# A hybrid decoder layer: the first piece of the input projections ordered by kinds of parts, and the keys' second copies made by DMA

## The chip, the core and the metric

The kernel runs on one core of a Trainium2 chip. A core has a matrix engine (TensorE, PE in the profile; PEld is its loading of weights), a vector engine (VectorE, DVE), an engine for activation functions (ScalarE, ACT), a general engine (GpSimd, POOL) and an engine that only issues transfers (SyncE, SP). Each takes its instructions in a fixed order and waits at semaphores for the others. ACT, POOL and SP issue DMA transfers, which all run on the same 16 DMA engines. Matrix products go to PSUM, which is divided into banks of 128 x 512 words; the other data lie in SBUF, 128 partitions wide.

The metric is the time of one execution on the device in microseconds (us); smaller is better. A change is compared with the kernel before on the same chip.

## What is computed

One layer with 1024 tokens, 16 learned meta tokens ahead of them, model width 1024, in float32. Cut to what matters here:

```python
u = rmsnorm(h, g_pre_mix)                   # h: 1040 x 1024
z = u @ w_in
q, k, v, xr, yr = jnp.split(z, [512, 640, 768, 1280], axis=-1)
attn = sliding_window_attention_with_sinks(q, k, v, sinks)    # 8 heads of 64, 2 key heads, window 128
xr = causal_depthwise_conv(xr, conv_w, conv_b)
rec = gelu(yr) * rg_lru(xr, ...)            # gates, then a recurrence over the tokens
h = h + rmsnorm(concat([attn, rec]) @ w_out, g_post_mix)
f = square(relu(rmsnorm(h, g_pre_ffn) @ w_ff1)) @ w_ff2       # width 4096
out = (h + rmsnorm(f, g_post_ffn))[16:]
```

## The kernel before

**Products in parts.** Every float32 operand of a product is split into a high part (a reduced float32 that PE multiplies quickly) and a low part (what is left). A product is then three matmuls: high by high, high by low, low by high. `mm3` (L121) issues the three in a row for each chunk of 128 of the inner dimension: L123, L124 and L125 in the profile. The high part is made by ACT (L95 for weights, L116 for u), the low part by DVE from the source and the high part (L98, L117), so DVE's instruction always follows ACT's.

**The opening.** The 1040 rows come in four blocks, `ALL` (L218): 272 columns of the transposed activations, then three of 256. For a block, `norm_rows` (L197) squares each tile of 128 rows on ACT (L200), POOL adds epsilon and takes the power -0.5 (L158, L164), and DVE scales the rows (L202). `transposed` (L235) transposes the scaled rows on PE (L242) chunk by chunk, eight chunks, into banks of three kinds (pt, o, s; two of each), and splits each chunk into the high and low parts of u (L116, L117). Then four projections with 128 output columns follow (L349 to L352): K, V, the first Q pair and the first X chunk. `project` (L205) runs 24 matmuls into a bank of kind acc, of which there are two, and a sink empties it. The key's sink `put_k` (L300) does for each of the two key heads: the high part on ACT (L303), a second copy of it on the other 64 partitions on DVE (L304), and the low part on DVE (L305). The scores need the high part on both halves, since the stationary operand holds q's high part on one half and q's low part on the other (L447, L451). The meta tokens' keys are kept apart in `km`; the other keys lie in `khh` (high, both halves) and `kl` (low, with the other half set to zero by POOL at L298).

**After it.** Scores and softmax (`scores`, L432: L467 and L480 on DVE, L82 on ACT) and the use of the values (`attend`, L486) run for four Q pairs and two halves of the tokens. The remaining projections (`fill_q`, `fill_x`, `fill_y`) are put between them with a lower priority, so that PE has work while a softmax runs. Then come the gates and the recurrence, the output projection, and the feed-forward part with seven products in place of eight.

**What sets the order.** The program is written in order of priority, and a planner that runs before the kernel is built turns it into one fixed list of instructions for each engine: it takes, by its own estimate of the times, the ready instruction of the highest priority. `behind` (L105) adds an order between two instructions of one engine without a semaphore. A tile of a kind (`slot`, `bank`) waits for an earlier tile of that kind to be done with.

Of the kernel before, what the change touches and what calls it, by code (L numbers as in the profile page):

```python
# [10 lines left out]
F32R = mybir.dt.float32r  # L11
AF = mybir.ActivationFunctionType
ALU = mybir.AluOpType
# [3 lines left out]
P = 128  # L17
D = 1024
KC = D // P
# [18 lines left out]
def hybrid_layer(  # L38
# [30 lines left out]
    def f32(ap):  # L69
        return ap.bitcast(F32)  # L70
# [34 lines left out]
    def behind(name, *inss):  # L105
        for ins in inss:
            tc.add_manual_dep(
                ins, name,
                mybir.DependencyInfo(
                    mybir.DependencyClass.NoSync, mybir.DependencyReason.DATA  # L110
                ),
                reason="order",
            )

    def split_scaled(hi, lo, src, scale):
        nc.scalar.activation(hi, src, AF.Copy, scale=scale)  # L116
        nc.vector.scalar_tensor_tensor(  # L117
            lo, src, scale, f32(hi), op0=ALU.mult, op1=ALU.subtract
        )

    def mm3(dst, lhs, rhs, start, stop):  # L121
        (lh, ll), (rh, rl) = lhs, rhs
        nc.tensor.matmul(dst, lh, rh, start=start, stop=False, skip_group_check=True)  # L123
        nc.tensor.matmul(dst, lh, rl, start=False, stop=False, skip_group_check=True)  # L124
        nc.tensor.matmul(dst, ll, rh, start=False, stop=stop, skip_group_check=True)  # L125


    ident = const.tile([P, P], F32, name="ident")
# [26 lines left out]
    def rstd_of(ssq_parts, n=P):  # L155
        ms = small.tile([P, 1], F32, name="ms", tag="ms")
        if len(ssq_parts) == 1:
            nc.gpsimd.tensor_scalar(ms[:n], ssq_parts[0], EPS, None, op0=ALU.add)  # L158
        else:
            nc.vector.scalar_tensor_tensor(  # L160
                ms[:n], ssq_parts[0], EPS, ssq_parts[1], op0=ALU.add, op1=ALU.add
            )
        rs = small.tile([P, 1], F32, name="rs", tag="rs")
        nc.gpsimd.tensor_tensor(rs[:n], ms[:n], half_pow[:n], op=ALU.pow)  # L164
        return rs[:n]


    def load_cols(cols, tag="ws"):
# [25 lines left out]
    u = [pair("a", [P, TT]) for _ in range(KC)]  # L194
    RMS_SC = 1.0 / math.sqrt(D)

    def norm_rows(src, n):  # L197
        xn = slot("d", [P, D])
        ssq = small.tile([P, 1], F32, name="ssq", tag="ssq")
        nc.scalar.activation(xn[:n], src, AF.Square, scale=RMS_SC, accum_out=ssq[:n])  # L200
        rs = rstd_of([ssq[:n]], n)
        nc.vector.tensor_scalar(xn[:n], src, rs, None, op0=ALU.mult)  # L202
        return xn

    def project(w, pieces, sink):  # L205
        wh, wl = w
        for t0, n in pieces:
            acc = bank("acc")
            for kc in range(KC):
                uh, ul = u[kc]  # L210
                mm3(
                    acc[:, :n], (wh[:, kc, :], wl[:, kc, :]),
                    (uh[:, t0 : t0 + n], ul[:, t0 : t0 + n]),
                    kc == 0, kc == KC - 1,
                )
            sink(acc[:, :n], t0, n)

    ALL = [(0, 272), (272, 256), (528, 256), (784, 256)]  # L218
    REAL2 = [(16, 512), (528, 512)]

    zero = slot("ws", [P, 512])
    nc.vector.memset(zero, 0.0)
# [12 lines left out]
    def transposed(b, xn):  # L235
        t0, n = ALL[b]
        for kc in range(KC):
            flip[0] += 1
            pt = bank(("pt", "o", "s")[flip[0] % 3])
            o = 0  # L240
            for s, m in xn:
                nc.tensor.transpose(  # L242
                    pt[:, o : o + m], s[:m, kc * P : (kc + 1) * P], ident[:m, :m]
                )
                o += m
            uh, ul = u[kc]
            split_scaled(
                uh[:, t0 : t0 + n], ul[:, t0 : t0 + n], pt[:, :n],
                g_mix_col[:, kc : kc + 1],
            )  # L250

    def fetch(cols, tag="raw"):
        raw = slot(tag, [P, KC, P])
# [20 lines left out]
    rx = fetch([(X_COL, P)], "e")  # L274
    for i in range(4, 8):
        load_x(i)
    wk = split_w(rk, "b")
    wv = split_w(rv, "b")
    transposed(0, xn)
    wq = split_w(rq)  # L280
    wx = split_w(rx)
    nsink = const.tile([P, 8], F32, name="nsink")
    nc.sync.dma_start(nsink, attn_sinks[0].partition_broadcast(P))
    prm_r = slot("d", [8, 512])
# [2 lines left out]
        nc.sync.dma_start(prm_r[4 + i : 5 + i, :], src)  # L287

    khh = [slot("b", [P, T], F32R) for _ in range(2)]
    kl = [slot("b", [P, T], F32R) for _ in range(2)]

    vk = [slot("b", [P, 8, P], F32R) for _ in range(2)]
    HALF = (slice(0, HD), slice(HD, P))
    vt = slot("c", [P, TT])
    for h in range(2):
        nc.gpsimd.memset(f32(kl[h][HALF[1 - h]]), 0.0)  # L298

    def put_k(hh, lo, src):  # L300
        for h in range(2):
            r, o = HALF[h], HALF[1 - h]
            nc.scalar.copy(hh[h][r], src[r])  # L303
            nc.vector.tensor_copy(hh[h][o], src[r])  # L304
            nc.vector.tensor_tensor(lo[h][r], src[r], f32(hh[h][r]), op=ALU.subtract)  # L305

    def sink_k(acc, t0, n):
        o = 0
        if t0 == 0:
            m = slice(0, NMETA)  # L310
            put_k(
                [km[:, 0, m], km[:, 1, m]], [km[:, 2, m], km[:, 3, m]], acc[:, m]
            )
            o = NMETA
        c = slice(t0 + o - NMETA, t0 - NMETA + n)
        put_k(
            [khh[0][:, c], khh[1][:, c]], [kl[0][:, c], kl[1][:, c]], acc[:, o:]
        )

    def sink_v(acc, t0, n):  # L320
        nc.scalar.copy(vt[:, t0 : t0 + n], acc)

    def new_q():

        q = pair("b", [P, T])

        def sink_q(acc, t0, n):
            c = slice(t0 - NMETA, t0 - NMETA + n)
            for h in range(2):
                r, o = HALF[h], HALF[1 - h]  # L330
                split_scaled(q[h][r, c], q[h][o, c], acc[r], HD ** -0.5)

        return q, sink_q

    def new_x(tag="d"):
# [4 lines left out]

        return xr, sink_x

    q0, sink_q0 = new_q()
# [938 lines left out]
```

## Time and profile before

| what | value |
|---|---|
| median of 3 runs | 973.48 us (972.43 to 975.89) |
| the profiled execution | 972.95 us |
| span of its profile, first to last instruction | 971.1 us |
| PE busy | 953.7 us, 98% |
| DVE busy | 674.6 us, 69% |
| ACT busy | 502.0 us, 52% |
| POOL busy | 82.4 us, 8% |
| granted clock of PE | 0.999 |

The span is 1.85 us shorter than the execution's own time. A row of the timeline gives the start and the length of an instruction in us, the engine, the line of the code, the operation, what it writes and reads, and the shapes; in square brackets stands how long its engine was idle before it and what ended that. A matmul's length includes the way through the array, so the distance between two starts tells its cost in a stream. PE counts as busy at whatever rate it runs.

### The profile page before, as it was taken

To read this page: it belongs to the slowest core of one execution; us is meant where nothing else is said; L and a number is where in the kernel's file an instruction comes from. 1 tells how busy PE (TensorE), PEld (TensorE's weight loads), DVE (VectorE), ACT (ScalarE), POOL (GpSimd) and SP (SyncE) were. 2 spreads that over 40 slices of the span, in tenths; PEclk is the share of its full clock that TensorE was granted. 3 is DMA by queue.
4 is the path that set the end of the run, shared out by engine and by line. 5 is a ranking of instruction groups with operands and counts; after the bars stand their busy time and mean duration, and the time that the engine had idled before them with its cause. 6 is when DMAs were issued, how large, how long until landed. Compare 5 with 4: busy or idle time off the path is not lost.

```text
span 971.1 us, 12490 instructions
## 1 busy us (share of the span) xinstructions
PE 953.7 (98%) x4782; PEld 803.0 (83%) x4782; DVE 674.6 (69%) x997; ACT 502.0 (52%) x809; POOL 82.4 (8%) x109
## 2 busy tenths in 40 slices
PE   6999999999999999999999999999999999999997
PEld 6999999888878887888888878888888888888786
DVE  6679997775976686665645465468557676779694
ACT  6646673567844554343555556555433344445350
POOL 4100000000002100000000000000111000003152
PEclk9999999999999999999999999999999999999999
DMA  9002001012234466576522264323678765548923
GB/s 296 23 1 66 23 23 44 23 48 64 84 119 144 159 207 209 173 251 209 198 87 87 97 206 125 114 87 114 172 176 198 186 224 187 184 163 195 223 80 87
DMA packets 88219, 130.13 MB, mean 134 GB/s; under 512 B 13624, under 2 KB 52552, under 8 KB 88160
## 3 DMA queue, kind: packets, MB, share of 16 engines
q1 hardware_dynamic: 79792, 107.33, 33.4%
q0 software_dynamic: 7792, 20.45, 10.1%
q10 hardware_dynamic: 576, 1.57, 0.4%
q8 instruction: 37, 0.61, 0.2%
q14 instruction: 22, 0.18, 0.1%
HBM read 110.46 MB, written 18.87 MB: 133 GB/s over the span
## 4 chain that ended last, share of the span: by engine, by line
PE 89%; DVE 4%; DMA 3%; issue 2%; ACT 1%; POOL 0%; SPq 0%; POOLq 0%; DVEq 0%; ACTq 0%
PE ps_acc L124 11%; PE ps_acc L123 11%; PE ps_acc L125 11%; PE ps_s L125 6%; PE ps_pt L123 6%; PE ps_s L124 6%; PE ps_pt L125 6%; PE ps_s L123 6%; PE ps_pt L124 6%; PE ps_o L124 5%; PE ps_o L123 5%; PE ps_o L125 5%; PE ps_o L506 2%; PE ps_pt L495 1%; DMA raw<-in_w_ff_dram 1%
## 5 line engine op out<-in xcount | busy, mean ns | idle before, releaser
L95 ACT CAST ws<-raw 128x1024 fp32r<-128x1024 f32 (+1 forms) x69 | 70.7, 1024 | 126.6 <-PE ps_o L124 48.8
L98 DVE TENSOR_TENSOR ws<-raw,ws 128x1024 fp32r<-128x1024 f32 (+1 forms) x70 | 83.5, 1194 | 59.6 <-ACT ws L95 59.5
L123 PE MATMUL ps_acc<-a,ws 128*128 128x256 f32 (+2 forms) x272 | 90.5, 333 | 0.6 <-DVE b L305 0.6
L124 PE MATMUL ps_acc<-a,ws 128*128 128x256 f32 (+2 forms) x272 | 89.8, 330 | 0.0
L125 PE MATMUL ps_acc<-a,ws 128*128 128x256 f32 (+2 forms) x272 | 89.4, 329 | 0.0
L98 DVE TENSOR_TENSOR b<-b,b 128x1024 fp32r<-128x1024 f32 (+2 forms) x48 | 57.6, 1201 | 24.7 <-PE ps_o L124 17.1
L95 ACT CAST ws<-e 128x1024 fp32r<-128x1024 f32 x43 | 45.0, 1046 | 55.3 <-PE ps_o L124 28.1
L95 ACT CAST b<-b 128x1024 fp32r<-128x1024 f32 (+2 forms) x48 | 49.4, 1030 | 42.8 <-DVE b L788 40.0
L98 DVE TENSOR_TENSOR ws<-e,ws 128x1024 fp32r<-128x1024 f32 x43 | 52.6, 1222 | 21.6 <-ACT ws L95 21.6
L123 PEld LDWEIGHTS ps_acc<-a,ws 128*128 128x128 f32 x272 | 51.2, 188 | 4.9 <-DVE b L305 0.8
L125 PEld LDWEIGHTS ps_acc<-a,ws 128*128 128x128 f32 x272 | 51.2, 188 | 4.6
L124 PEld LDWEIGHTS ps_acc<-a,ws 128*128 128x128 f32 x272 | 51.2, 188 | 3.9
L164 POOL TENSOR_TENSOR rs<-ms,half_pow 128x1 f32<-128x1 f32 (+1 forms) x31 | 21.3, 692 | 356.5 <-DVE ms L160 355.1
L123 PE MATMUL ps_acc<-ws,b 128*128 128x512 f32 (+1 forms) x120 | 46.3, 386 | 0.4 <-ACT ws L95 0.4
L124 PE MATMUL ps_acc<-ws,b 128*128 128x512 f32 (+1 forms) x120 | 46.5, 388 | 0.2 <-DVE ws L98 0.2
L125 PE MATMUL ps_acc<-ws,b 128*128 128x512 f32 (+1 forms) x120 | 46.2, 385 | 0.0
L123 PE MATMUL ps_pt<-ws,b 128*128 128x512 f32 x112 | 44.1, 394 | 0.0
L124 PE MATMUL ps_pt<-ws,b 128*128 128x512 f32 x112 | 44.1, 394 | 0.0
L125 PE MATMUL ps_pt<-ws,b 128*128 128x512 f32 x112 | 44.0, 393 | 0.0
L123 PE MATMUL ps_s<-ws,b 128*128 128x512 f32 x110 | 43.4, 395 | 0.0
L124 PE MATMUL ps_s<-ws,b 128*128 128x512 f32 x110 | 43.3, 393 | 0.0
L125 PE MATMUL ps_s<-ws,b 128*128 128x512 f32 x110 | 43.3, 393 | 0.0
(381 smaller groups left out, 2690.1 us busy)
## 6 DMA issues: line engine op xcount, KB each, us to landing
raw<-in_w_ff_dram SPq DMA_DIRECT2D x62, 512.0 KB, 4.0
e<-in_w_ff_dram SPq DMA_DIRECT2D x45, 512.0 KB, 3.6
d<-in_w_ff_dram SPq DMA_DIRECT2D x12, 512.0 KB, 3.8
s_dram<-d POOLq DMA_DIRECT2D x12, 512.0 KB, 3.9
raw<-in_w_in_dram SPq DMA_DIRECT2D x9, 512.0 KB, 3.6
c<-in_x_dram SPq DMA_DIRECT2D x8, 512.0 KB, 8.5
d<-in_x_dram SPq DMA_DIRECT2D x8, 512.0 KB, 4.6
out_dram<-raw SPq DMA_DIRECT2D x8, 512.0 KB, 2.6
```

What stands on the lines that cost most here:

```text
L95: nc.scalar.copy(hi, src)
L98: low = nc.vector.tensor_tensor(lo, src, f32(hi), op=ALU.subtract).ins
L123: nc.tensor.matmul(dst, lh, rh, start=start, stop=False, skip_group_check=True)
L124: nc.tensor.matmul(dst, lh, rl, start=False, stop=False, skip_group_check=True)
L125: nc.tensor.matmul(dst, ll, rh, start=False, stop=stop, skip_group_check=True)
L164: nc.gpsimd.tensor_tensor(rs[:n], ms[:n], half_pow[:n], op=ALU.pow)
L495: nc.tensor.transpose(pt[:, o : o + P], sn[h][:, 2 * bp + i, s * P : (s + 1) * P], ident,)
L506: nc.tensor.matmul(po[:, oc : oc + n], v, p_[:, pc : pc + n], start=first and k == 0, stop=last and k == 1, skip_group_check=True,)
```

## The change

In the first block the four projections no longer run chunk by chunk. A new function `part` issues the eight matmuls of one kind for a block: kind 0 is high by high, 1 is high weights by low u, 2 is low weights by high u. K and V run kinds 0 and 1 first; kind 2 of K and of V follows later; Q and X run the three kinds in turn.

The instructions of ACT and of DVE in this part are put in a written order with `chained` (0 for ACT, 1 for DVE). ACT: wk's high part, the eight high parts of u, the high parts of wv and wq, the square of the third row tile, K's high parts, the square of the fourth row tile, V's copy, wx's high part. DVE: the eight low parts of u, the low parts of wk, wv and wq, the third row tile's scaling, K's low parts, the fourth row tile's scaling, wx's low part.

The second copies of the keys' high parts leave the sink; after the loop over the blocks four transfers on POOL's queue make them for all tokens and for the meta tokens. The sinks of K and Q do both heads on ACT and then both on DVE. The tiles `khh` and `kl` and their memsets stand ahead of the first rows in the program. The transpositions of the third and fourth block are put behind the last matmul of the first and second block, and the memset of the gate weights behind the last power of a norm.

```diff
+    def part(acc, w, piece, k, last=2):
+        t0, n = piece
+        for kc in range(KC):
+            last_mm[0] = nc.tensor.matmul(
+                acc[:, :n], w[k // 2][:, kc, :], u[kc][k % 2][:, t0 : t0 + n],
+                start=k == 0 and kc == 0, stop=k == last and kc == KC - 1,
+                skip_group_check=True,
+            ).ins.name
...
+    khh = [slot("b", [P, T], F32R) for _ in range(2)]
+    kl = [slot("b", [P, T], F32R) for _ in range(2)]
+    HALF = (slice(0, HD), slice(HD, P))
+    for h in range(2):
+        nc.gpsimd.memset(f32(kl[h][HALF[1 - h]]), 0.0)
...
+    def chained(e, ins):
+        if last[e] is not None:
+            behind(last[e], ins)
+        last[e] = ins.name
+
+    def high_w(raw, tag="ws"):
+        hi, lo = pair(tag, [P, KC, P])
+        chained(0, nc.scalar.copy(hi, raw).ins)
+        return hi, lo
+
+    def low_w(w, raw):
+        chained(1, nc.vector.tensor_tensor(w[1], raw, f32(w[0]), op=ALU.subtract).ins)
...
-    wk = split_w(rk, "b")
-    wv = split_w(rv, "b")
+    wk = high_w(rk, "b")
     transposed(0, xn)
-    wq = split_w(rq)
-    wx = split_w(rx)
+    low_w(wk, rk)
+    wv = high_w(rv, "b")
+    low_w(wv, rv)
+    wq = high_w(rq)
+    low_w(wq, rq)
...
-    def put_k(hh, lo, src):
-        for h in range(2):
-            r, o = HALF[h], HALF[1 - h]
-            nc.scalar.copy(hh[h][r], src[r])
-            nc.vector.tensor_copy(hh[h][o], src[r])
-            nc.vector.tensor_tensor(lo[h][r], src[r], f32(hh[h][r]), op=ALU.subtract)
+    def high_k(hh, src):
+        return [nc.scalar.copy(hh[h][HALF[h]], src[HALF[h]]).ins for h in range(2)]
+
+    def low_k(hh, lo, src):
+        return [
+            nc.vector.tensor_tensor(
+                lo[h][HALF[h]], src[HALF[h]], f32(hh[h][HALF[h]]), op=ALU.subtract
+            ).ins
+            for h in range(2)
+        ]
...
     for b in range(4):
         if b:
-            transposed(b, normed(b))
-        piece = [ALL[b]]
-        project(wk, piece, sink_k)
-        project(wv, piece, sink_v)
-        project(wq, piece if b else [(16, 256)], sink_q0)
-        project(wx, piece, sink_x0)
+            transposed(b, xn if b == 1 else normed(b), done[b])
+        piece = ALL[b]
+        if b == 0:
+            acc = [bank("acc"), bank("acc")]
+            for a, w in zip(acc, (wk, wv)):
+                part(a, w, piece, 0)
+                part(a, w, piece, 1)
+            xn = [(norm_rows(xt[2], P, True), P)]
+            part(acc[0], wk, piece, 2)
+            sink_k(acc[0][:, : piece[1]], *piece)
+            xn.append((norm_rows(xt[3], P, True), P))
+            part(acc[1], wv, piece, 2)
+            sink_v(acc[1][:, : piece[1]], *piece)
+            wx = high_w(rx)
+            low_w(wx, rx)
+            for w, (t0, n), sink in ((wq, (16, 256), sink_q0), (wx, piece, sink_x0)):
+                acc = bank("acc")
+                for k in range(3):
+                    part(acc, w, (t0, n), k)
+                sink(acc[:, :n], t0, n)
+            done.append(last_mm[0])
+            continue
+        project(wk, [piece], sink_k)
+        project(wv, [piece], sink_v)
+        project(wq, [piece], sink_q0)
+        project(wx, [piece], sink_x0)
+        done.append(last_mm[0])
+    for h in range(2):
+        r, o, m = HALF[h], HALF[1 - h], slice(0, NMETA)
+        nc.gpsimd.dma_start(f32(khh[h][o]), f32(khh[h][r]))
+        nc.gpsimd.dma_start(f32(km[o, h, m]), f32(km[r, h, m]))
...
-    nc.gpsimd.memset(graw, 0.0)
+    behind(last_pow[0], nc.gpsimd.memset(graw, 0.0).ins)
```

More of the change, by code (lines that the diff above doesn't have):

```diff
@@ L115, in split_scaled @@
     def split_scaled(hi, lo, src, scale):
-        nc.scalar.activation(hi, src, AF.Copy, scale=scale)
-        nc.vector.scalar_tensor_tensor(
+        high = nc.scalar.activation(hi, src, AF.Copy, scale=scale).ins
+        low = nc.vector.scalar_tensor_tensor(
             lo, src, scale, f32(hi), op0=ALU.mult, op1=ALU.subtract
-        )
+        ).ins
+        return high, low
     def mm3(dst, lhs, rhs, start, stop):
@@ L233, in normed, with transposed @@
         return [(norm_rows(s[:m], m), m) for s, m in rows]
-    def transposed(b, xn):
+    last = [None, None]
+    def chained(e, ins):
[8 more added lines that the diff above has]
+        chained(1, nc.vector.tensor_tensor(w[1], raw, f32(w[0]), op=ALU.subtract).ins)
+    def transposed(b, xn, after=None):
         t0, n = ALL[b]
@@ L241, in transposed @@
             for s, m in xn:
-                nc.tensor.transpose(
+                ins = nc.tensor.transpose(
                     pt[:, o : o + m], s[:m, kc * P : (kc + 1) * P], ident[:m, :m]
                 )
+                if after:
+                    behind(after, ins.ins)
                 o += m
             uh, ul = u[kc]
-            split_scaled(
+            high = split_scaled(
                 uh[:, t0 : t0 + n], ul[:, t0 : t0 + n], pt[:, :n],
@@ L250, in transposed @@
             )
+            if b == 0:
+                chained(0, high[0])
+                chained(1, high[1])
     def fetch(cols, tag="raw"):
@@ L341, in new_x @@
         return xr, sink_x
+    done = [None, None]
     q0, sink_q0 = new_q()
```

69 lines of the change are left out of this document (46 added, 23 removed).

## The prediction

> **What bounds the kernel now.** I read the page's busy line first, then the windows of the first 60 us, then the list of what PE waited for.
>
> ```profile
> span 971.1 us, 12490 instructions
> PE 953.7 (98%) x4782; PEld 803.0 (83%) x4782; DVE 674.6 (69%) x997; ACT 502.0 (52%) x809; POOL 82.4 (8%) x109
> ...
> 0.00:30.00 30.00, 21.43 (x132) 19.91 (x133) 21.29 (x42) 21.84 (x44) 12.16 (x31) 1.00 0.81 257
> 30.00:60.00 30.00, 30.00 (x258) 29.79 (x257) 19.49 (x66) 15.23 (x41) 2.73 (x5) 1.00 0.01 2
> ...
> PE ps_s L242 <- DVE d L202: 5.8, 1, 5.8
> PE ps_o L242 <- DVE a L117: 0.7, 1, 0.7
> ...
> PE ps_acc L123 <- DVE b L305: 0.6, 1, 0.6
> ```
>
> The windows' columns are the stretch, its length, then busy time of PE, PEld, DVE, ACT, POOL. PE is idle for 17.4 us of the span (971.1 - 953.7), and half of that, 8.57 us, lies in the first 30 us; in the next 30 it is never idle. So PE sets the end, and what the opening loses is lost for good. The first wait ends at the normalised rows (L202), the next at a low part of u that is late (L117, bank of a transposition), the last at the key's sink (L305, accumulator bank).
>
> Idle time isn't the whole loss. In the timeline (start, length, engine, line) of the opening:
>
> ```profile
> 8.40 1.52 DVE L202 TENSOR_SCALAR d<-c,rs 128x1024 f32<-128x1024 f32 x1 [0.77 <-POOL rs L164]
> 8.43 2.38 POOL L298 MEMSET b<- 64x1024 f32 x2
> 9.85 2.34 DVE L98 TENSOR_TENSOR b<-raw,b 128x1024 fp32r<-128x1024 f32 x2
> 10.49 0.49 ACT L116 ACTIVATE a<-ps_o,gcol 128x272 fp32r<-128x272 f32 x1
> 11.62 0.50 ACT L116 ACTIVATE a<-ps_o,gcol 128x272 fp32r<-128x272 f32 x1
> 12.11 0.49 DVE L117 SCALAR_TENSOR_TENSOR a<-ps_o,gcol,a 128x272 fp32r<-128x272 f32 x1
> 12.52 0.49 DVE L117 SCALAR_TENSOR_TENSOR a<-ps_s,gcol,a 128x272 fp32r<-128x272 f32 x1
> 15.40 0.57 PE L124 MATMUL ps_acc<-a,b 128*128 128x272 f32 x1
> 17.32 0.75 DVE L202 TENSOR_SCALAR d<-c,rs 128x1024 f32<-128x1024 f32 x1
> 18.95 0.43 PE L124 MATMUL ps_acc<-a,b 128*128 128x272 f32 x1
> 19.18 0.36 PE L125 MATMUL ps_acc<-a,b 128*128 128x272 f32 x1
> 25.71 0.28 PE L123 MATMUL ps_acc<-a,ws 128*128 128x256 f32 x1
> 25.83 0.28 PE L124 MATMUL ps_acc<-a,ws 128*128 128x256 f32 x1
> 28.32 0.29 PE L124 MATMUL ps_acc<-a,ws 128*128 128x272 f32 x1
> 31.05 0.29 PE L125 MATMUL ps_acc<-a,ws 128*128 128x272 f32 x1
> 31.18 0.27 PE L242 MATMUL ps_pt<-ident,d 128*128 128x128 f32 x1
> 31.29 0.27 PE L242 MATMUL ps_o<-ident,d 128*128 128x128 f32 x1
> ```
>
> Three things. The L202 at 8.40 takes 1.52 us instead of 0.75 (17.32), beside the memsets of the low key tiles on POOL. The low parts of wk and wv (L98 x2, 2.34 us) stand on DVE ahead of the first low part of u (12.11), so PE's second product of the first chunk waits. And matmuls of 272 columns start 0.23 us apart up to 19.18 (from 18.95), but 0.124 apart later (22 steps from 28.32 to 31.05; the step comes at 19.4): PE runs at half rate until 4.0 us after its stream became unbroken at 15.40.
>
> **The change part by part.** I follow dates, since each engine feeds the next.
>
> (a) The memsets move ahead of the first rows, where POOL is waiting for data; then that L202 ends at 8.40 + 0.75 = 9.15 rather than 9.92. If POOL's mask work, pushed back by them, falls beside L202 instead, the 0.77 is not gained. I take the gain, as POOL's whole displaced 2.4 us fit into the opening's idle POOL time (30 - 12.2 us).
>
> The Trainium skill, "SBUF — State Buffer" (section on the two separate sides), says that GpSimd and a two-port VectorE instruction exclude each other for a whole instruction. The trace's 1.52 against 0.75 agrees. By the same page's warning in that section, copies issued from GpSimd's queue can also be held up by such VectorE instructions; by it each of the four issues could lose up to one such instruction, which the cover in (f) holds off the sum only if they are short.
>
> (b) ACT makes the eight high parts of u in one run. The first came 0.57 us after the rows were ready (10.49 - 9.92), so now at 9.72; a step is 0.38 us (10.49 to 11.62 in three); the eighth ends at 9.72 + 7 x 0.38 + 0.49 = 12.9. DVE follows with the low parts at 0.41 steps (12.11 to 12.52) from about 10.3, so the banks for the last two chunks come free in time, and the eighth low part ends at 13.7. K's eight high-by-high products end at 13.1.
>
> (c) From 13.1 PE has K's second eight, then V's sixteen; wv's high part (on ACT, as wide as the square of 1.06 us below) ends at 14.0, its use starts at 14.9. When does the fast rate come? Counting 4.0 us from 13.1, at 17.1; counting from the first product at 10.3, at 14.3. K's first eight fill some 60% of that stretch (8 x 0.23 of 2.9 us), so I take 16.4. Up to there 8 + 3.3/0.23 = 22 of the 48 products of K and V are done, the other 26 take 26 x 0.124 = 3.2: K and V end at 19.6, K alone at 18.7. Low weights are no bar: DVE has wk's at 14.9, wv's at 16.1, wq's at 17.3 (2.34 / 2 = 1.2 us each), and K needs its at 17.7.
>
> The Trainium skill, "TensorE: Matmul & The Clock Gate" (Part 1), puts the rate down to a gate that looks at free-running windows of some 3.4 us. The trace's 4.0 us agrees; windows counted back from 19.3 would put the step at 15.9, 0.2 us better than mine, and where they lie differs from run to run.
>
> (d) The rest of the piece. K's sink is four ACT and four DVE instructions, and between it and V's copy stands the squaring of the next rows:
>
> ```profile
> 15.17 1.06 ACT L200 ACTIVATE d<-c 128x1024 f32<-128x1024 f32 x1 [0.97 <-PE ps_s L242]
> 16.14 0.19 ACT L200 ACTIVATION_READ_ACCUMULATOR d<-c 128x1 f32 x1
> ...
> L303 ACT CAST km<-ps_acc x2: 167/168/168, 21.9 to 22.9; 64x16 fp32r<-64x16 f32 x2
> ...
> L304 DVE CAST b<-ps_acc 64x256 fp32r<-64x256 f32 x8 | 3.4, 422 | 2.3 <-ACT b L303 2.2
> ...
> L303 ACT CAST b<-ps_acc 64x256 fp32r<-64x256 f32 x8 | 2.9, 368 | 5.8 <-DVE b L305 3.9 <-PE ps_acc L125 1.9
> ```
>
> ACT: highs to 19.8 (2 x 0.37 + 2 x 0.17), square to 21.1, V's copy to 21.5, wx's high part to 22.5. DVE: K's lows to 20.3, the rows 1.0 us after their square (17.32 - 16.33) to 22.8, wx's low part to 24.0. PE: six transpositions meanwhile, Q at 20.3 for 24 x 0.12 = 2.9 to 23.2, X from 23.2 (its high part is 0.7 us early, its low part is wanted at 25.2) to 26.2. That 0.7 us is the thinnest cover of the fixed order: an ACT run later than that delays X one for one. Ten transpositions are left, 1.1 us at 0.11 each, and K of the second piece then waits about 0.6 us for its first high and low parts (two of about 0.5 us in a row, less the transpositions beside them): 27.9.
>
> Before, X ended at 31.18 with 20 of these transpositions done, four beyond the second block's 16: 31.18 - 0.4 = 30.8. The gain is 30.8 - 27.9 = **2.9 us**, and as PE isn't idle in the next 30 us it is carried on. Bounds: fast rate at 14.3 gives 0.9 more, at 19.2 as before 1.3 less; no gain in (a) 0.77 less; the wait of 0.6 gone, 0.6 more, or doubled, 0.6 less.
>
> (e) Eight DVE copies of 0.42 us and two of 0.17 go (L304). They gave PE only the 0.6 us wait, which is in (d); elsewhere PE's other accumulator covers them. The memset of the gate weights moved behind the last norm, and the order put on transpositions, cost nothing: the gates run after 200 us.
>
> (f) The copies come back as four transfers on POOL's queue, behind the highs of piece four. The nearest rows are those of the transfers to s_dram, twice the size (issue in ns, landing in us):
>
> ```profile
> L833 POOL DMA_DIRECT2D s_dram<-d x12: 531/531/782, 350.6 to 475.0; - x12
> ...
> DMA to landing us min/median/max: 3.0/3.9/5.7
> ...
> 60.11 0.28 PE L123 MATMUL ps_acc<-a,b 128*128 128x256 f32 x1
> 72.75 0.28 PE L125 MATMUL ps_acc<-a,ws 128*128 128x256 f32 x1
> ```
>
> All scores now wait for them. Before, 24 score matmuls (12 each on L447 and L451) and four transpositions of scores ran before X of piece four ended at 72.9; without them and with the gain it ends at 72.9 - 24 x 0.12 - 0.5 - 2.9 = 66.6. K of that piece ends at 60.11 + 2.9 - 2.9 - 16 x 0.12 = 58.2, its highs at 59.0; four issues of 0.53 and 3.9 us give 65.0 (64.1 to 66.8 by the extremes). V, Q and X cover that; without the cover the copies would cost 6.8 us. What is late next is the softmax of the first half pair, below.
>
> The sum: the profiled execution took 972.95 (span 971.1), less 2.9 is 970.05; the median of 973.48 stands 0.53 above that execution, so **970.5**.
>
> **The rivals.** *A larger gain.* The fast rate at 14.3 and no wait at piece two: 2.9 + 0.9 + 0.6 = 4.4, 969.1. For it: K's early products. Against: they leave gaps.
>
> *A smaller one.* Mask work beside L202 (0.77) and a late rate step (17.1 rather than 16.4, 0.3), or ACT's chain 1 us later than X allows: gain 1.8, 971.7.
>
> *Slower: the softmax is pushed into the stretch where DVE is full.* The work that DVE did on the first scores before 73 us (4.37 us on L467, 2.28 on L480) now follows the copies:
>
> ```profile
> 52.00:73.00 21.00, 4.37 (x20) 1.00 0.01 2
> ...
> 52.00:73.00 21.00, 2.28 (x8) 1.00 0.01 2
> ...
> 73.00:112.00 39.00, 36.83 (x107) 1.00 0.16 42
> 112.00:150.00 38.00, 34.43 (x88) 1.00 0.11 29
> 150.00:200.00 50.00, 37.33 (x85) 1.00 0.15 43
> ```
>
> DVE is idle for only 2.2 of the 39 us from 73, then 3.6 of 38, then 12.7 of 50. It decides if PE has no projections left to fill with before DVE has caught up, near 150 us: then 6.65 us of waiting less the 2.9 make 3.8 slower, 977.3. Against it: the projections don't depend on the scores, PE can do them first, and DVE's room up to 200 us is 18.4 us.
>
> **How the numbers follow.** No change at all and 0.3% (2.9 us) are what a measurement can just tell apart. Forecast 0.52, its own range 969.3 to 972.0, a little more than half of it beyond 2.9 us (0.29 against 0.23); larger gain 0.15; smaller 0.15; slower 0.18. So faster by over 0.3% is 0.29 + 0.15 = 0.44, within 0.3% 0.23 + 0.15 = 0.38, slower 0.18. The range runs from 968.6 (the larger gain and 0.5 of spread) to 975.8, well into the slower case.
>
> **What would show it.** Right: the L202 of the second rows near 0.75 us; the fast rate before 17.5 us; X of the first piece ending near 26; no wait on L305; PE at full time from 30 to 270 us; copies landing before X of piece four ends. Wrong: PE waiting on scores between 66 and 200 us, an ACT instruction of the fixed order waiting while PE stands, or the rate step still near 19.

## The result, and the profile after

The changed kernel is slower: 978.52 us median (976.15 to 981.89) against 974.40 us for the kernel before in the same comparison, a ratio of 1.004 with a 95% interval of 1.0023 to 1.0057. One of its eleven executions took 1922.17 us at a granted clock of 1.0; it is left out of the range and the ratio, and nothing on record tells why it took twice as long. The loss is about 4.1 us, where 3.0 us faster was forecast. Its profiled execution took 978.91 us (span 977.1 us, mean granted clock 0.996).

The busy line of its page:

```profile
span 977.1 us, 12511 instructions
PE 955.6 (98%) x4782; PEld 802.3 (82%) x4782; DVE 670.4 (69%) x987; ACT 503.2 (51%) x809; POOL 84.7 (9%) x113
```

PE is idle for 21.5 us, 4.1 us more than before. What it waited for (in all, how often, the longest):

```profile
PE ps_o L153 <- POOL mask L474: 6.5, 1, 6.5
PE ps_acc L124 <- ACT d L407: 2.1, 1, 2.1
PE ps_acc L125 <- DVE ws L98: 1.7, 2, 1.5
...
PE ps_o L602 <- ACT c L95: 0.6, 1, 0.6
...
PE ps_acc L237 <- DVE km L355: 0.5, 1, 0.5
```

The first line is the start of the opening, before any rows are ready.

And the windows (stretch, its length, busy time of PE, PEld, DVE, ACT, POOL, then granted clock, DMA share, GB/s):

```profile
30.00:60.00 30.00, 29.88 (x256) 29.45 (x255) 15.88 (x43) 14.80 (x38) 4.42 (x8) 1.00 0.05 10
...
112.00:150.00 38.00, 37.39 (x301) 36.28 (x299) 34.55 (x93) 26.35 (x68) 0.00 (x0) 1.00 0.10 29
150.00:200.00 50.00, 47.88 (x282) 42.51 (x283) 38.07 (x94) 24.82 (x60) 0.00 (x0) 0.97 0.11 33
```

DVE has less to do in the stretch from 30 to 60 us (15.88 us busy, before 19.49), in part because the scores now come later. The wait of 0.6 us on the key's sink (L305) is gone, but the first piece now waits 0.5 us on the same sink (L355, at 21.29 us). But a wait of 2.1 us that the kernel before doesn't have now stands at L124, and the stretch from 150 to 200 us has 2.1 us of PE idle and a lower clock. The timeline of that place (start, length, engine, line; in brackets the idle time ahead and what ended it):

```profile
149.92 0.33 PE L602 MATMUL ps_o<-c,vm 128*128 128x128 f32 x1 [0.61 <-ACT c L95]
...
151.86 1.29 DVE L631 SCALAR_TENSOR_TENSOR d<-d,prm,d 128x1037 f32<-128x1037 f32 x1
...
153.19 0.66 ACT L407 COPY d<-ps_acc 128x272 f32<-128x272 f32 x2 [0.88 <-DVE d L631]
...
153.63 0.55 PE L124 MATMUL ps_acc<-a,ws 128*128 128x256 f32 x1 [2.08 <-ACT d L407]
```

Its windows, with the same columns as above:

```profile
152.00:154.00 2.00, 0.37 (x2) 0.38 (x3) 2.00 (x4) 0.97 (x3) 0.00 (x0) 0.92 0.00 0
154.00:156.00 2.00, 2.00 (x11) 2.00 (x11) 2.00 (x7) 0.00 (x0) 0.00 (x0) 0.50 0.04 8
156.00:158.00 2.00, 2.00 (x15) 2.00 (x15) 0.14 (x1) 0.00 (x0) 0.00 (x0) 0.72 0.00 0
```

Read it backwards. PE needs an accumulator bank; the bank is freed by ACT's copy of the X projection (L407); ACT waits for a buffer of the ring d; that buffer is held by the convolution of the chunk before (L631, 1.29 us), on a DVE that is busy without a gap (2.00 of 2.00 us). Why DVE is behind there is what e8 below tells. After the wait PE runs at half rate for some 3 us (granted clock 0.50). Lost here: 0.61 + 2.08 us of idle, and by the clock an estimated 2 x (0.08 + 0.50 + 0.28) = 1.7 us, some 4.4 us in all.

Three dates show where the time goes: the matmul that waited for ACT's L971 (L1067 in the changed kernel), a weight's cast in the feed-forward part, and an eviction late in it. First the kernel before, then the changed one:

```profile
365.08 0.50 PE L123 MATMUL ps_acc<-b,ws 128*128 128x512 f32 x1 [0.68 <-ACT a L971]
509.50 1.05 ACT L95 CAST ws<-raw 128x1024 fp32r<-128x1024 f32 x1 [2.43 <-PE ps_o L124]
825.39 0.60 ACT L1191 ACTIVATE a<-ps_acc 128x512 f32<-128x512 f32 x1 [0.26 <-PE ps_acc L125]
```

```profile
367.31 0.49 PE L124 MATMUL ps_acc<-b,ws 128*128 128x512 f32 x1 [0.68 <-ACT a L1067]
512.78 1.05 ACT L95 CAST ws<-raw 128x1024 fp32r<-128x1024 f32 x1 [2.46 <-PE ps_o L125]
831.26 0.60 ACT L1287 ACTIVATE a<-ps_acc 128x512 f32<-128x512 f32 x1 [0.29 <-PE ps_acc L126]
```

At the first date the changed kernel is 2.2 us late. It loses another 1.05 us to the second and 2.6 us to the third, in stretches in which PE has few waits (1.5 us near 780 us is the longest): so there are two causes at least. All runs by the same three dates (us against the first profile of before), with the shift of the first exp of the softmax, PE's idle time from 146 to 160 us, and the mean distance between the starts of neighbouring matmuls of 512 columns from 30 to 135 us behind the first date (some 450 of them):

| kernel | first exp | idle 146-160 | date 1 | date 2 | date 3 | distance | ratio (95%) |
|---|---|---|---|---|---|---|---|
| before, second profile | 0.0 | 0 | -0.1 | -0.1 | -0.4 | 0.2305 | - |
| after | +15.8 | 2.7 | +2.2 | +3.3 | +5.9 | 0.2321 | 1.004 (1.0023-1.0057) |
| after, second profile | +15.2 | 2.7 | +2.9 | +3.8 | +5.3 | 0.2321 | - |
| e1 | +11.5 | 2.1 | +3.4 | +4.3 | +5.9 | 0.2318 | 1.0044 (1.003-1.0058) |
| e2 | +11.0 | 2.1 | +1.4 | +2.5 | +3.9 | 0.2318 | 1.0033 (1.002-1.0046) |
| e3 | +17.7 | 1.4 | +3.1 | +3.1 | +5.2 | 0.2305 | 1.0033 (1.0021-1.0044) |
| e5 | +3.2 | 0 | -3.1 | -2.0 | -1.2 | 0.2314 | 0.9997 (0.9986-1.0008) |
| e6 | +10.3 | 2.1 | +2.5 | +3.1 | +4.3 | 0.2314 | 1.0044 (1.003-1.0058) |
| e7 | +5.1 | 0 | -0.7 | +0.3 | 0.0 | 0.2305 | 1.0003 (0.999-1.0016) |
| e8 | +17.5 | 2.0 | +2.4 | +2.4 | +2.5 | 0.2305 | 1.0028 (1.0014-1.0041) |
| e9 | +3.0 | 0 | -3.3 | -2.0 | -1.6 | 0.2314 | 0.9994 (0.9984-1.0004) |
| e10 | +0.4 | 0 | -0.1 | +0.8 | +1.8 | 0.2315 | 1.0007 (0.9989-1.0024) |
| e12 | +5.3 | 0 | -0.7 | +0.1 | +0.7 | 0.2308 | 1.0 (0.9982-1.0018) |

### The profile page after: what moved, and what is told of

It is laid out like the page before. It is cut to its first block, busy times and chain, and to the rows that moved or that the text cites. A ratio compares the mean times of both kernels' runs of the same rounds, so it can differ in the third digit from the quotient of the medians.

```text
span 977.1 us, 12511 instructions
## 1 busy us (share of the span) xinstructions
PE 955.6 (98%) x4782; PEld 802.3 (82%) x4782; DVE 670.4 (69%) x987; ACT 503.2 (51%) x809; POOL 84.7 (9%) x113
## 4 chain that ended last, share of the span: by engine, by line
PE 88%; DVE 5%; DMA 3%; issue 2%; ACT 2%; POOL 0%; POOLq 0%; DVEq 0%; SPq 0%; ACTq 0%
PE ps_acc L125 10%; PE ps_acc L124 10%; PE ps_acc L126 10%; PE ps_s L126 6%; PE ps_pt L124 6%; PE ps_s L125 6%; PE ps_pt L125 6%; PE ps_s L124 6%; PE ps_pt L126 6%; PE ps_o L125 5%; PE ps_o L124 5%; PE ps_o L126 5%; PE ps_o L602 2%; PE ps_pt L591 1%; PE ps_acc L237 1%
## 5 line engine op out<-in xcount | busy, mean ns | idle before, releaser
L95 ACT CAST ws<-raw 128x1024 fp32r<-128x1024 f32 (+1 forms) x69 | 70.7, 1024 | 126.7 <-PE ps_o L125 56.0
L98 DVE TENSOR_TENSOR ws<-raw,ws 128x1024 fp32r<-128x1024 f32 (+1 forms) x70 | 83.5, 1192 | 52.6 <-ACT ws L95 52.5
L124 PE MATMUL ps_acc<-a,ws 128*128 128x256 f32 (+2 forms) x256 | 86.6, 338 | 2.2 <-ACT d L407 2.1
L125 PE MATMUL ps_acc<-a,ws 128*128 128x256 f32 (+2 forms) x256 | 85.7, 335 | 0.0
L126 PE MATMUL ps_acc<-a,ws 128*128 128x256 f32 (+2 forms) x256 | 85.6, 335 | 0.0
L98 DVE TENSOR_TENSOR b<-b,b 128x1024 fp32r<-128x1024 f32 (+2 forms) x48 | 57.6, 1199 | 28.1 <-PE ps_o L125 20.5
L95 ACT CAST ws<-e 128x1024 fp32r<-128x1024 f32 x41 | 42.8, 1044 | 57.1 <-PE ps_o L125 41.1
L95 ACT CAST b<-b 128x1024 fp32r<-128x1024 f32 (+2 forms) x48 | 49.4, 1030 | 40.1 <-DVE b L884 37.4
L98 DVE TENSOR_TENSOR ws<-e,ws 128x1024 fp32r<-128x1024 f32 x41 | 50.1, 1222 | 15.7 <-ACT ws L95 15.7
L124 PEld LDWEIGHTS ps_acc<-a,ws 128*128 128x128 f32 x256 | 49.1, 192 | 6.5 <-ACT d L407 2.3
L126 PEld LDWEIGHTS ps_acc<-a,ws 128*128 128x128 f32 x256 | 48.9, 191 | 4.5
L125 PEld LDWEIGHTS ps_acc<-a,ws 128*128 128x128 f32 x256 | 49.0, 191 | 3.7
L124 PE MATMUL ps_acc<-ws,b 128*128 128x512 f32 (+1 forms) x120 | 46.3, 386 | 0.0
L124 PE MATMUL ps_pt<-ws,b 128*128 128x512 f32 x112 | 44.2, 395 | 0.0
L124 PE MATMUL ps_s<-ws,b 128*128 128x512 f32 x110 | 43.5, 395 | 0.0
```

Source lines behind the costliest of these rows:

```text
L95: nc.scalar.copy(hi, src)
L98: low = nc.vector.tensor_tensor(lo, src, f32(hi), op=ALU.subtract).ins
L126: last_mm[0] = nc.tensor.matmul(dst, ll, rh, start=False, stop=stop, skip_group_check=True).ins.name
```

## The experiments

**e1: the second copies by DVE again, all else as changed.** In the key's sink of the changed kernel, behind its low parts, and without the four transfers:

```
+            ops[1] += [
+                nc.vector.tensor_copy(hh[h][HALF[1 - h]], src[HALF[h]]).ins
+                for h in range(2)
+            ]
```

> The changed kernel with the second copies of the keys' high parts made by VectorE again in each piece (behind the low parts); the order of the first piece stays. Theory A (the scores that wait for the late copies push the softmax into a stretch where VectorE is full, and PE runs dry near 150 us): scores start before the fourth piece again, no stall of PE between 100 and 200 us, and the gain of the first piece of about 2 us remains: 1.5 to 3 us faster than the kernel before, 5 to 7 faster than the changed one. Rival B (the new order of the first piece itself leads the planner into a worse list): still 3 to 5 us slower than before, with the stall.

978.30 us median against 973.19. The late transfers are gone, and the wait of 2.0 us on the copy of X stays. The first exp is still 11.5 us late. So theory A, as far as it put the loss down to the late copies alone, fell.

**e2: the same transfers, each piece's in its own sink.**

```
+        for hh, lo, src in parts:
+            for h in range(2):
+                nc.gpsimd.dma_start(f32(hh[h][HALF[1 - h]]), f32(hh[h][HALF[h]]))
```

> The changed kernel with the same transfers for the second copies, but issued in each piece behind its own high parts, so that the first scores need only the first pieces. Theory A: as with VectorE's copies, 1.5 to 3 us faster than before, no stall near 150 us. Rival C (transfers on POOL's queue are what costs, wherever they stand): still 3 to 5 us slower than before.

977.49 us, the same wait (2.0 us), the first exp 11.0 us late. With e1 it says that late transfers aren't all that holds the scores back: PE's fixed order does too. In the trace of the kernel before, the first score on khh is PE's 324th matmul; in e2 it is the 423rd, and in the changed kernel, where the scores wait for the late transfers as well, the 475th. My reading, which e5 supports: in the kernel before the planner found gaps ahead of piece four's projections and put scores there; with the quicker opening it finds none, and the scores come behind them by rank.

**e3: the transfers alone, behind the last piece, in the kernel before.**

```
-            nc.vector.tensor_copy(hh[h][o], src[r])
...
+    for h in range(2):
+        r, o, m = HALF[h], HALF[1 - h], slice(0, NMETA)
+        nc.gpsimd.dma_start(f32(khh[h][o]), f32(khh[h][r]))
+        nc.gpsimd.dma_start(f32(km[o, h, m]), f32(km[r, h, m]))
```

> The kernel before with only the second copies moved into transfers behind the last piece; the first piece chunk by chunk as before. Theory A: 4 to 7 us slower than before, with a wait of PE on a sink or a softmax between 100 and 200 us. Rival B: within 1 us of before.

977.30 us against 973.19, a loss without the new opening too, 3.1 us of it by the first date. Its waits are others: 0.69 us at 124 us, 0.92 and 0.40 us near 156 us, on the split of the softmax's results (L95, L98) and not on the copy of X. From the first to the second date nothing is added: the second cause isn't here. Of the 2.1 us that come by the third date, 1.7 are waits for the low parts of weights (0.34 us at 716 us, 1.35 at 779), on which more below.

**b0: the kernel before, profiled again.**

> The kernel before once more, for a second profile of it. In the feed-forward part (370 to 660 us) the changed kernel fell back by another 1.4 us although both lists should be alike there. If that is how executions differ, the second profile of before differs from the first by as much; if it belongs to the change, the two profiles of before agree within 0.3 us there.

Span 970.6 us; it keeps within 0.1 us of the first profile to the second date and within 0.4 us to the third. A shift of 1 us from the first date to the second, as in both profiles of the changed kernel (1.05 and 0.95 us), is thus hardly an accident of one execution.

**e5: scores first.** The kernel e2, with the projections of piece four ranked behind the first scores:

```
+        with deferred(LATE if b == 3 else 0):
             project(wk, [piece], sink_k)
...
```

> The changed kernel with the transfers issued in each piece, and the four projections of the last piece put behind the first scores in the planner's priority (500 places later). The runs before showed that whatever makes the copies, the first scores came 11 to 18 us late wherever the sinks or the first piece left PE no planned gaps, and that all of these have PE stalls near 150 us. Theory A2 (the late start of the softmax is what costs, whoever delays it): the first softmax starts before 56 us, no wait of PE between 100 and 200 us, date at the gates 2 us or more before that of the kernel before, 0.5 to 3 us faster than before in all. Rival B2 (the first piece's order itself makes the later list worse, the date of the scores doesn't matter): the stall near 150 us stays, 3 to 4 us slower than before.

972.68 us against 972.89. The windows of e5, in which the first score on khh is PE's 374th matmul:

```profile
73.00:112.00 39.00, 39.00 (x276) 36.27 (x275) 34.54 (x97) 24.31 (x65) 0.00 (x0) 1.00 0.13 36
112.00:150.00 38.00, 38.00 (x296) 36.56 (x295) 35.90 (x91) 25.39 (x62) 0.00 (x0) 1.00 0.16 41
150.00:200.00 50.00, 50.00 (x298) 44.09 (x298) 37.62 (x85) 23.29 (x56) 0.00 (x0) 1.00 0.13 36
```

PE is never idle from 73 to 200 us, at full clock, and the opening's gain is there at the first date (3.1 us). Each against the kernel before in its own comparison, e2 is 4.3 us slower and e5 0.2 us faster: order alone is worth 4.5 us. But of those 3.1 us half is gone at the end of the span (969.6 against 971.1). This execution is also the fastest of its twelve (971.34 us). In the median nothing is won against the kernel before, where 0.5 to 3 us were expected.

**e6 and e7: the tiles khh and kl and their memsets at the old place in the program**, in e2 and in e5.

```
-    khh = [slot("b", [P, T], F32R) for _ in range(2)]
-    kl = [slot("b", [P, T], F32R) for _ in range(2)]
...
     vk = [slot("b", [P, 8, P], F32R) for _ in range(2)]
```

> The changed kernel with the transfers issued in each piece, and the tiles of the keys (khh, kl) and their memsets back at their old place in the program, behind wk and wv. It is for the slow drift: from 364 to 500 us the changed kernel and its two variants lose another 1.0 us against before (matmuls 0.2325 us apart instead of 0.2305), the old first piece with late copies loses nothing. Theory P (where the tiles lie in SBUF makes the matmul stream slower, and the early tiles of the keys moved them): no drift from 364 to 500 us, 1 to 2 us faster than the variant with early tiles, and the second rows' scaling back at 1.5 us. Rival Q (the drift belongs to what is left of the first piece): drift of 1.0 us as before, same time.

> Both edits together: scores first, and the key tiles at their old place. Theory A2 with P: no stall near 150 us and no drift, 2 to 4 us faster than the kernel before. A2 with Q: the same time as with scores first alone. B2: 2 us slower than before or more.

977.07 and 973.16 us: no gain in either, and the wait stays in e6. By the dates the expectation seemed to fall, since both lose about as much from the first to the second date as before (0.7 and 1.0 us). The distances tell more: 0.2305 us again in e7, whose loss is an early step and not a steady one. In e6 it is 0.2314: by the list in e10's expectation, its tiles of the ring b lie elsewhere all the same. In e7 the memsets are beside the second rows again, which take 1.52 us, so part of the opening's gain is gone too.

**e8: late scores alone.** The kernel before, no transfer, the eight DVE copies kept; the first scores ordered behind the last product of X of piece four:

```
+    piece_end = last_mm[0]
...
+                    if j == 0 and half == 0:
+                        behind(piece_end, first.ins)
```

> The kernel before, with one thing changed: the first score matmuls (first half pair) are ordered on PE behind the last matmul of X of piece four. No DMA copy, the eight copies by DVE stay, the first piece is untouched. Theory A2 (the late start of the softmax is by itself what costs, since DVE has no room between 73 and 150 us and PE runs out of projections near 150 us): a PE wait of 1 to 3 us between 145 and 160 us, the gates 2.5 to 4 us later than in the kernel before, total 975.5 to 977.5 with no gain of the first piece to set against it, ratio 1.0025 to 1.0045. Rival C (the transfers, or the order of the keys' sinks, cost something that the late start of the scores alone does not): within 1 us of the kernel before, no wait between 140 and 160 us.

976.09 us against 973.17. The timeline of e8:

```profile
155.08 0.38 PE L123 MATMUL ps_acc<-a,ws 128*128 128x256 f32 x1 [2.02 <-ACT d L343]
...
154.64 0.66 ACT L343 COPY d<-ps_acc 128x272 f32<-128x272 f32 x2 [0.87 <-DVE d L542]
```

The same chain at the same place, with no other part of the change: bank, copy of X, convolution. The late start of the softmax costs about 2.9 us by itself; here no half rate follows, and nothing more is lost at the later dates.

**e9: e5, with the two mask memsets behind the first rows' power.**

```
+    behind(first_pow, nc.gpsimd.memset(mask, 0.0).ins)
```

> The kernel e5_scores_first with POOL's two mask memsets ordered behind the first power of the first rows (L164 in the kernel before), so that no mask work lies ahead of the rows. If the 0.63 us of mask work that was seen ahead of the power is what made the first rows ready at 9.8 rather than 9.15 us, the rows are ready near 9.15, the X of the first piece ends 0.5 to 0.7 us earlier, and all that is carried: total 971.5 to 972.3, ratio 0.998 to 0.9995. Rival: DVE's chain or ACT's chain absorbs it (the rate step comes no earlier), X of the first piece within 0.2 us of e5 and the total as in e5, 972.7.

972.87 us against 973.17. The rows are ready at 8.29 + 0.92 = 9.21 us, as forecast in (a), but the first date moves by only 0.2 us against e5, so the rival came out:

```profile
8.29 0.92 DVE L216 TENSOR_SCALAR d<-c,rs 128x1024 f32<-128x1024 f32 x1 [0.77 <-POOL rs L170]
```

**e10: other places alone.** The kernel before, with khh and kl requested ahead of the first load; every engine has the same instructions in the same order.

```
+    khh = [slot("b", [P, T], F32R) for _ in range(2)]
+    kl = [slot("b", [P, T], F32R) for _ in range(2)]
     zero = slot("ws", [P, 512])
```

> The kernel before with only the places of tiles in SBUF changed: the tiles khh and kl are requested where the changed kernel requests them, ahead of the first load, and nothing else. Every engine has the same instructions in the same order as in the kernel before; all of the tiles of the ring b that the matmuls of 512 columns after 365 us read lie elsewhere. So far the spacing of those matmuls was 0.2305 us in every kernel whose b tiles lie as before (the two profiles of before, e3, e7, e8) and 0.2312 to 0.2322 in those where they lie elsewhere (after, e1, e2, e5, e6, e9). Theory P2 (the places set the spacing): spacing 0.2312 to 0.2322 between 395 and 500 us, the wait behind L971 within 0.3 us of 365.1, but the L1191 that comes at 825.39 in the profile of before 1 to 2.5 us later; total 1 to 2 us more, ratio 1.001 to 1.002. Rival: something else in the new opening does it (the order on ACT, the transfers); then 0.2305, all dates within 0.3 us of before, ratio 1.000.

The same three dates, in e10:

```profile
365.01 0.50 PE L123 MATMUL ps_acc<-b,ws 128*128 128x512 f32 x1 [0.68 <-ACT a L971]
510.29 1.05 ACT L95 CAST ws<-raw 128x1024 fp32r<-128x1024 f32 x1 [2.44 <-PE ps_o L124]
827.18 0.60 ACT L1191 ACTIVATE a<-ps_acc 128x512 f32<-128x512 f32 x1 [0.29 <-PE ps_acc L125]
```

Equal at the first date, 0.8 us late at the second, 1.8 at the third, and a span of 973.8 us against 971.1; the distance is 0.2315 us. So the second cause is shown: where the tiles lie in SBUF sets how closely the matmuls that read them follow each other. It accounts for the step to the second date; of the 1.0 us from there to the third, 0.71 is a wait at 759 us for the low part of a weight, whose transfer landed late. In the medians (975.32 against 974.22) it is 1.1 us, which the interval doesn't separate from none.

**e12: e9, with the ring b back in its old region.** First tiles of the rings ws and raw, and wk's and wv's, are requested ahead of khh; again no engine's order changes.

```
+    zero = slot("ws", [P, 512])
+    first_raw = slot("raw", [P, KC, P])
+    pk, pv = pair("b", [P, KC, P]), pair("b", [P, KC, P])
     khh = [slot("b", [P, T], F32R) for _ in range(2)]
```

> The kernel e9_scores_first_masks_late with the first tiles of the rings ws and raw and the pairs of wk and wv requested ahead of khh and kl, so that the ring b lies in the same region of SBUF as in the kernel before, though two of its buffers are rotated; every engine has the same instructions in the same order as in e9. Of the first 590 matmuls of 512 columns, 156 read a b tile from another place than before, against all 590 in e9. Theory P2: spacing about 0.2305 to 0.2310 between 395 and 500 us instead of 0.2314; 3.0 to 3.3 us ahead of the kernel before at 365 us as in e9, and most of it kept to the end: span 968.0 to 968.8 against 969.6, total 971.0 to 972.2, ratio 0.9975 to 0.999, faster than both kernels. Rival (places don't matter): as e9, span 969.6, total 972.9.

973.43 us against 974.22; missed. The distance fell as expected (0.2308), but this execution was 2.5 us behind e9 by the first date, from the opening: its first rows were there 0.6 us later (their square starts at 5.23 us, in e9 at 4.62), and the fast rate came later too. Windows of the opening, of the changed kernel and then of e12 (PE's busy time, its matmuls in brackets, granted clock, DMA share, GB/s):

```profile
14.00:15.00 1.00, 0.96 (x8) 1.00 0.99 351
15.00:16.00 1.00, 1.00 (x11) 1.00 1.14 345
16.00:17.00 1.00, 1.00 (x11) 1.00 1.10 427
```

```profile
15.00:16.00 1.00, 1.00 (x7) 1.00 1.10 343
16.00:17.00 1.00, 1.00 (x6) 1.00 1.17 415
17.00:18.00 1.00, 1.00 (x10) 1.00 1.02 414
```

The count of matmuls per microsecond shows the fast rate from near 14.5 us in the one and from 17 in the other. Counted in the same way it came between 13.0 and 14.5 in e1, e5, e6 and e9, and near 16 in e2 and e7. The Trainium skill, "TensorE: Matmul & The Clock Gate" (Part 1), says that the gate looks at free-running windows, so that the step varies from run to run; these executions agree, with a spread of 4 us in the step. The start of PE's stream explains only a part: in the changed kernel, e2 and e12 the first product starts alike, at 11.06 to 11.07 us, and the step comes near 14.5, 16.5 and 17.

**a1: the changed kernel, profiled again.**

> The changed kernel itself, a second profiled execution, to see which of the losses belong to the kernel and which to one execution. Lost for good if they belong to the kernel: the wait of PE near 153.6 us on the ACT copy L407 (2.1 us), the half rate behind it, the spacing of 0.2317 to 0.2322 us in the matmuls of 512 columns after 395 us, and the wait on DVE's low parts near 780 us (1.5 us). What differs between the two, by over 0.3 us, is a matter of the execution; the opening (rows ready at 9.80, K's high parts from 18.77) is expected within 0.6 us, as transfers from memory may land at other times.

978.37 us in one run. Of its list of waits:

```profile
PE ps_acc L124 <- ACT d L407: 2.1, 1, 2.1
PE ps_acc L125 <- DVE ws L98: 0.9, 2, 0.7
```

And its windows:

```profile
152.00:154.00 2.00, 1.00 (x4) 1.00 (x5) 2.00 (x7) 0.66 (x2) 0.00 (x0) 0.58 0.00 0
154.00:156.00 2.00, 2.00 (x12) 2.00 (x11) 1.51 (x4) 0.00 (x0) 0.00 (x0) 0.50 0.03 8
156.00:158.00 2.00, 2.00 (x11) 2.00 (x11) 0.00 (x0) 0.00 (x0) 0.00 (x0) 0.50 0.00 0
158.00:160.00 2.00, 2.00 (x15) 2.00 (x14) 0.00 (x0) 0.17 (x1) 0.00 (x0) 0.71 0.00 0
```

The wait, the half rate and the wide distance (0.2321) belong to the kernel. How long the half rate lasts (here some 7 us) and the wait of 1.5 us on DVE near 780 us (here 0.7) differ between executions.

## Why the prediction was wrong, and where it was right

The step that failed is the end of (d): that the gain is carried on "as PE isn't idle in the next 30 us". (f) named "What is late next" rightly, the softmax, but priced it as a rival only. The slower rival had the place (near 150 us) and the mechanism (softmax pushed into the stretch where DVE is full), and got a chance of 0.18. That its size comes close (3.8 us slower, measured 4.1) is luck: PE waited 2.7 us there and not 6.65, and the half rate, the places of the tiles and a late transfer, none of which it had, made up the rest. The argument set against it, that "PE can do them first, and DVE's room up to 200 us is 18.4 us", was wrong in two ways. Most of that room lies behind the wait: 12.7 of the 18.4 us come after 150 us. And projections do depend on DVE: an X projection's bank is freed by ACT's copy into a buffer of the ring d, which the convolution on DVE still reads. That chain was in the kernel before, and following "acc" from the projection to its sink would have shown it.

(a) Half right. The second rows take 0.75 us as forecast. When the first rows' square starts, in the kernel before:

```profile
4.73 1.06 ACT L200 ACTIVATE d<-c 128x1024 f32<-128x1024 f32 x1 [0.76 <-DMA c<-in_x_dram]
```

And the timeline of the changed kernel:

```profile
5.38 1.06 ACT L209 ACTIVATE d<-c 128x1024 f32<-128x1024 f32 x1 [1.38 <-DMA c<-in_x_dram]
...
5.72 0.63 POOL L474 TENSOR_SCALAR_AFFINE_SELECT mask<-mask 128x16 f32<-128x16 f32 x1
6.61 0.23 POOL L163 TENSOR_SCALAR ms<-ssq 128x1 f32<-128x1 f32 x1 [0.26 <-ACT d L209]
...
9.05 0.75 DVE L215 TENSOR_SCALAR d<-c,rs 128x1024 f32<-128x1024 f32 x1 [0.77 <-POOL rs L169]
...
13.82 0.49 ACT L116 ACTIVATE a<-ps_s,gcol 128x272 fp32r<-128x272 f32 x1 [0.57 <-PE ps_s L291]
...
18.77 0.74 ACT L351 CAST b<-ps_acc 64x256 fp32r<-64x256 f32 x2 [1.53 <-PE ps_acc L237]
```

The second rows start at 9.05 instead of 8.40 and are ready at 9.80, where 9.15 was forecast. In this execution the input is the reason: the first rows landed 0.65 us later, and POOL, done with its displaced mask work at 6.35, waited 0.26 us for ACT's square of them. Where the rows land early the mask work does cost: e5 and e9 start the square at 4.65 and 4.62 us, and the second rows start at 8.82 in e5 and at 8.29 in e9, which has the mask work behind. So some 0.5 of the 0.77 us can go to it: "the opening's idle POOL time" was long enough for the mask work, and the place was the wrong one. (b) The step of ACT is 0.37 us (0.38), but the eighth high part waits for PE's transposition and ends at 14.3, not 12.9. (c) The fast rate came near 14.5 in this execution, earlier than the 16.4 taken and inside its bounds; over all kernels with this opening it lay between 13 and 17, so 16.4 was a fair middle and one execution can't confirm it. (d) K's highs start at 18.77 (K was to end at 18.7), but that agreement is luck: the rows were 0.65 us late and the eighth high part 1.4, and the early rate step made up for it. Q starts at 21.29, not at 20.3, and X ends near 27.9, not at 26.2; the second piece begins right behind it, at 27.89, the date forecast, but four of its transpositions are still to come. At X of piece four, 67.93 us against the 66.6 forecast, the gain is 2.1 us of 2.9: the kernel before is there at 72.87 and has then done 20 scores of 0.12 us and four transpositions of 0.11 more (72.87 - 67.93 - 2.84). The smaller rival's 1.8 was nearer to the opening's worth than 2.9; e5's 3.1 at the first date is nearer to the forecast.

(e) Half right: the wait of 0.6 us at 28 us went with the DVE copies, but Q's start at 21.29 is a new wait of 0.5 us on the same sink. DVE, in the written order, scales the third row tile (19.01 to 19.77) ahead of K's low parts, and Q needs the bank that they read. (f) The transfers did what was forecast. What the trace has of those two issues:

```profile
L447 POOL DMA_DIRECT2D b<-b x2: 529/564/598, 60.1 to 60.7; - x2
...
DMA to landing us min/median/max: 2.9/3.3/3.7
```

And the timeline:

```profile
67.81 0.28 PE L126 MATMUL ps_acc<-a,ws 128*128 128x256 f32 x1
...
68.07 0.31 PE L543 MATMUL ps_s<-b,b 128*128 128x128 f32 x1
```

They land by about 64.4 (60.7 + 3.7), 3.5 us ahead of the end of X, and the scores start right behind it. The cover was counted on PE alone, which is the failed step seen from the other side; for the softmax, which had work from 53.8 us in the kernel before, it was no cover. The second cause has no term in the sum at all: that tiles come to lie elsewhere was not thought of.

The account of the profiled execution, by dates: opening -2.1 us at 68 us, 4.4 us lost near 150 us, +2.2 at the first date; then places, by e10 +0.9 to the second date and, without its wait, +0.3 to the third (after: 1.05, and 2.6 with a wait of 1.5 us on DVE near 780 us). That wait isn't the places' doing: a weight's transfer landed late, as the DVE rows of the kernel before and then of the changed one show.

```profile
769.65 1.23 DVE L788 TENSOR_TENSOR raw<-raw,e 128x1024 f32<-128x1024 f32 x1 [0.94 <-DMA e<-in_w_ff_dram]
```

```profile
777.18 1.23 DVE L884 TENSOR_TENSOR raw<-raw,e 128x1024 f32<-128x1024 f32 x1 [4.52 <-DMA e<-in_w_ff_dram]
```

In e3, with the old places, DVE waited 4.36 us there and PE 1.35. Why the transfer lands later in these kernels is open.

No version beat the kernel before by more than can be measured: e5, e7, e9 and e12 all lie within 0.1% of it, 4 to 5 us ahead of the changed kernel. In its profile e5 gives back 1.1 of the 3.1 us of the opening by the second date, where the places act, and 0.8 more by the third. That profile was a favourable execution, with an early rate step; in the medians nothing of the opening's gain is left. A version with both the early opening and exactly the old places was not found (e12 has most of them, and met a late rate step).

## What to carry to other kernels

A step hidden behind the bounding engine's work can still be dear if it starts another engine's chain later: ask how much room that engine has between the old start and the first place where the bounding engine needs it, and not over a longer stretch. With a planner, a quicker opening or a moved transfer changes which gaps exist, so look up where in the fixed order of PE the dependent work lands before pricing anything. And when a kernel drifts without waits, compare the distance of equal matmuls: an edit that requests tiles earlier moves others, hundreds of microseconds away.

## What the runs showed of the hardware

The distance between matmuls of 512 columns depends on where their operands lie: 0.2305 us in five profiles with the old places (before twice, e3, e7, e8) and 0.2314 to 0.2321 in those in which the tiles of the ring b lie elsewhere, with equal order on every engine in e10; in e12, where 156 of the first 590 such matmuls read a tile from another place, it is 0.2308. That is 0.4 to 0.7%, at a granted clock of 1.00; which relation of places is the good one stays open.

A wait of 2.0 to 2.1 us, with little work around it, was enough for half rate in the changed kernel (twice), e1 and e6 (granted clock 0.50 to 0.54 in the slowest 2 us behind it), and not in e2 and e8 (1.00). The Trainium skill, "TensorE: Matmul & The Clock Gate" (Part 1), puts the return to half rate at one idle window of about 3.4 us; here 2.7 us of idle between 149.3 and 153.6 us sufficed. In the opening, in contrast, the column of the granted clock reads 1.00 while matmuls run at half rate, so the count of matmuls per microsecond is the surer sign there.
